# An attention stage on Trainium2: row maxima as 64-row tile pairs, in batches at the borders of scores and values

## The chip, the cores and the metric

The kernel runs on one core of a Trainium2 chip. A core has a matrix engine (TensorE, PE in the profile; PEld is its weight load), VectorE (DVE), ScalarE (ACT), GpSimd (POOL) and SyncE (SP), which here issues nearly all DMAs. Each engine works through its own instructions in order and waits on semaphores for the others. Operands lie in SBUF (128 partitions); matmul results lie in eight PSUM banks of 512 float32 per partition, and a bank must have been read before another matmul may use it. The metric is the device time of one execution in microseconds.

## The reference

One layer of a diffusion transformer on 2048 latent tokens and 256 context tokens, width 1024, in float32:

```python
sh1, sc1, g1, sh2, sc2, g2 = split(silu(c) @ w_mod + b_mod, 6)
h_x = rmsnorm(x, norm1_g) * (1 + sc1) + sh1
p_x = h_x @ w_in                      # k, v, q, u, vg, gate_a, gate_b
k_x, q_x = rope(rmsnorm(k)), rope(rmsnorm(q)) * 64 ** -0.5
s = q @ [k_ctx, k_x].T                # 8 heads of 64, 2 key/value heads, 2304 keys
attn = softmax(s) @ [v_ctx, v_x]
gm = gelu(u) * (gm_ws @ rmsnorm(gelu(vg)) + gm_bs)
x = x + g1 * ((sigmoid(ga) * (attn @ w_br_attn) + sigmoid(gb) * (gm @ w_br_gm)) @ w_out)
x = x + g2 * (relu(h2 @ w_ff1) ** 2 @ w_ff2)   # h2: rmsnorm of x, modulated by sh2, sc2
```

The context is projected to keys and values alone.

## The kernel before

The stages follow one another: the first part of the modulation (sh1, sc1), the projection (`project`, four blocks b of 512 tokens, up to about 780 us), the attention (`attend`, to about 1545), the merge of the branches with `w_out` (to about 1860) and the feed-forward part.

**Numbers in two parts.** A float32 factor is split into a high part that the format fp32r holds and the remainder, and a product is made of three matmuls (L155 to L157); `split` casts the high part (L123 on ACT, L125 on VectorE) and subtracts (L127). Weights come by DMA on SP (L435 in the projection), are split, and are then used.

**A unit of the attention** is a block b and a pair of heads p: 512 queries, two heads, 2304 keys in 18 key tiles j of 128. Scores stand transposed, keys on the partitions. Two matmuls make a score tile: `KA` (high part of the keys in rows 0 to 63, remainder in rows 64 to 127) with `qa` (the queries' high part, twice; L815), and `KB` (the high part in rows 0 to 63, a row of ones in row 64, zeros) with `qb` (the queries' remainder, and in row 64 minus the query's maximum; L816). So the exp (L818 on ACT) needs no bias. The values are float32 matmuls of the exps with the head's values, one head in columns 0 to 63 and one in 64 to 127 of one bank `o` (L826). The exps are added up over the key tiles on VectorE and POOL (L841, 512 columns each; L846 joins the two), and 16 matmuls with a column of ones turn the result into sums (L858), whose reciprocals (L863) are transposed (L866), copied and stored (L869) for the merge. `oc`, a copy of `o` (L850), is stored unscaled.

**Maxima** must be known before a unit's first score: `attn_prep` makes them one unit ahead, 40 matmuls (four query tiles, two heads, five key blocks; L770), each with one reduce on VectorE (L774), then their joint maximum (L779), its negative (L780) and the transposes for `qb` (L161, copied at L791).

**Order.** `attend` goes through three groups of six key tiles; after each score tile of a unit come three steps of the next unit's `attn_prep`, behind a group the values of the group before. At every sixth key tile one step of `mod_rest` (g1, sh2, sc2, g2: loads L280, multiply-adds L287 on VectorE, matmuls with ones L299 and L315) is put in; these are pinned. At its end `order` makes each tile of a pool wait for the program's previous tile of that pool (pools and their sizes: `POOLS`) and, in the attention, holds TensorE to the program's order; all else is ordered by a scheduler. Unit 0's maxima are made in the projection's tail, one step behind each piece of its last block.

## Time and profile before

| | |
|---|---|
| times of three runs, us | 3271.23, 3276.57, 3291.97 (median 3276.57) |
| profiled execution | 3275.92 us, its span 3274.1 us, mean clock of TensorE 0.979 |
| busy share of the span | PE 96%, DVE 61%, ACT 41%, POOL 30% |
| exps (L818, tiles in `pt`) | 480, 603 ns each |
| reduces of the maxima (L774) | 640, 627 ns each |
| adds of the exps on POOL (L841) | 272 of the commonest form, 1410 ns each |
| value matmuls (L826), records | 960 of the commonest form, 613 ns each |

A row of a group gives line, engine, operation, output<-input, shapes and count, then busy time and the mean duration in ns of one, then the engine's idle time just before and what ended it. A row of the timeline starts with the time from the span's start and the duration in us; "x3" joins neighbours, "[1.66 <-PE b L770]" is idle time and what ended it. SPq rows are DMA issues on SP.

### The profile page before, as it was taken

How to read it: one execution, taken by the hardware profiler on the slowest of the kernel's cores; microseconds unless marked ns; L12 is line 12 of the kernel's file. 1: busy time of each engine (PE TensorE's matmuls, PEld its weight loads, DVE VectorE, ACT ScalarE, POOL GpSimd, SP SyncE). 2: the span in 40 equal slices, each digit the busy share in tenths (PEclk: the TensorE clock that was granted, in tenths of full speed). 3: DMA queues.
4: the chain of work that ended last, by engine and by line, in shares of the span. 5: the costliest groups of instructions: out<-in, count | busy, mean ns of one | idle time of the engine just before them, and what ended most of it. 6: DMA issues, size and time to landing. Idle time of an engine off the chain costs nothing.

```text
span 3274.1 us, 38611 instructions
## 1 busy us (share of the span) xinstructions
PE 3127.4 (96%) x14100; PEld 2397.0 (73%) x14100; DVE 1987.0 (61%) x2910; ACT 1353.3 (41%) x2034; POOL 982.9 (30%) x672
## 2 busy tenths in 40 slices
PE   8999999999999999998799988999999899999999
PEld 4888887887555666664587766888778688888777
DVE  4736354556787888774433339887754676664555
ACT  3343534343444544453322216444543344443333
POOL 1423233334777887777633310000000000000000
PEclk9999999999999999999899998999999999999999
DMA  6353534342111111001555536989655634445564
GB/s 201 98 193 107 169 118 152 114 139 83 49 49 52 46 33 52 26 11 43 183 177 173 163 111 228 313 308 312 220 202 197 220 137 158 145 149 195 209 218 170
DMA packets 331838, 484.79 MB, mean 148 GB/s; under 512 B 33920, under 2 KB 166144, under 8 KB 331648
## 3 DMA queue, kind: packets, MB, share of 16 engines
q1 hardware_dynamic: 326032, 481.98, 44.0%
q8 instruction: 110, 1.80, 0.2%
q10 hardware_dynamic: 5616, 0.35, 0.1%
q14 instruction: 80, 0.66, 0.1%
HBM read 347.97 MB, written 134.28 MB: 147 GB/s over the span
## 4 chain that ended last, share of the span: by engine, by line
PE 76%; DVE 10%; DMA 5%; POOL 3%; issue 3%; ACT 2%; SPq 1%; ACTq 0%; DVEq 0%; POOLq 0%
PE b L1176 11%; PE b L1177 11%; PE b L1175 11%; PE b L157 7%; PE b L156 7%; PE b L155 7%; PE b L826 7%; PE b L770 4%; PE b L815 3%; PE b L816 3%; DVE ts L774 2%; PE b L161 2%; DMA f<-w2o_d 1%; DMA w<-in_w_in 1%; DVE f L1270 1%
## 5 line engine op out<-in xcount | busy, mean ns | idle before, releaser
L774 DVE TENSOR_REDUCE ts<-b 128x1 f32<-128x512 f32 (+1 forms) x640 | 357.4, 627 | 153.5 <-PE b L770 153.3
L841 POOL TENSOR_TENSOR t<-t,pt 128x512 f32<-128x512 f32 x272 | 376.5, 1410 | 137.2 <-ACT pt L818 134.6
L1261 DVE TENSOR_TENSOR f<-f,f 128x1024 fp32r<-128x1024 f32 x224 | 272.8, 1224 | 235.1 <-ACT f L1260 230.7
L1260 ACT CAST f<-f 128x1024 fp32r<-128x1024 f32 x224 | 235.0, 1051 | 381.8 <-DMA f<-ao_d 287.7
L1176 PE MATMUL b<-f,f 128*128 128x512 f32 x896 | 354.1, 395 | 15.2 <-DVE f L1261 14.7
L1177 PE MATMUL b<-h,f 128*128 128x512 f32 x896 | 350.0, 391 | 9.1 <-DVE f L1132 7.2
L1175 PE MATMUL b<-h,f 128*128 128x512 f32 x896 | 350.3, 392 | 4.8 <-ACT f L1131 4.3
L818 ACT ACTIVATE pt<-b 128x512 f32<-128x512 f32 x480 | 257.9, 603 | 227.0 <-PE b L816 221.7
L1177 PE MATMUL b<-f,f 128*128 128x512 f32 x896 | 351.1, 392 | 0.0
L1176 PE MATMUL b<-h,f 128*128 128x512 f32 x896 | 349.9, 391 | 0.0
L1175 PE MATMUL b<-f,f 128*128 128x512 f32 x896 | 306.6, 396 | 22.2 <-ACT f L1260 20.6
L127 POOL TENSOR_TENSOR w<-w,w 128x1024 fp32r<-128x1024 f32 x60 | 146.8, 2447 | 388.3 <-ACT w L123 152.0
L815 PE MATMUL b<-t,t 128*128 128x512 f32 x576 | 238.1, 413 | 0.0
L816 PE MATMUL b<-t,t 128*128 128x512 f32 x576 | 226.8, 394 | 0.0
L826 PE MATMUL b<-pt,t 128*64 128x512 f32 x960 | 223.3, 613 | 0.0
L123 ACT CAST w<-w 128x1024 fp32r<-128x1024 f32 x120 | 125.9, 1049 | 225.7 <-DMA w<-in_w_in 197.9
L1175 PEld LDWEIGHTS b<-f,f 128*128 128x128 f32 x896 | 168.7, 190 | 64.5 <-ACT f L1260 26.0
L1176 PEld LDWEIGHTS b<-f,f 128*128 128x128 f32 x896 | 169.8, 189 | 59.8 <-DVE f L1261 25.0
L155 PE MATMUL b<-t,w 128*128 128x512 f32 x512 | 203.2, 397 | 1.0 <-DVE t L568 1.0
L1177 PEld LDWEIGHTS b<-h,f 128*128 128x128 f32 x896 | 169.0, 189 | 45.9 <-DVE f L1132 7.9
L157 PE MATMUL b<-t,w 128*128 128x512 f32 x512 | 200.6, 392 | 0.0
L156 PE MATMUL b<-t,w 128*128 128x512 f32 x512 | 200.6, 392 | 0.0
(212 smaller groups left out, 6249.4 us busy)
## 6 DMA issues: line engine op xcount, KB each, us to landing
w<-in_w_in SPq DMA_DIRECT2D x120, 512.0 KB
ao_d<-f SPq DMA_DIRECT2D x224, 256.0 KB
f<-ao_d SPq DMA_DIRECT2D x112, 512.0 KB
f<-w2o_d SPq DMA_DIRECT2D x112, 512.0 KB
f<-in_w_ff SPq DMA_DIRECT2D x48, 1024.0 KB
w2o_d<-f SPq DMA_DIRECT2D x112, 256.0 KB
t<-in_w_mod SPq DMA_DIRECT2D x32, 512.0 KB
f<-x_d SPq DMA_DIRECT2D x64, 256.0 KB
```

What stands on the lines that cost most here:

```text
L155: mm(ps, sh, mh, start=start, stop=False)
L156: mm(ps, sh, ml, start=False, stop=False)
L157: mm(ps, sl, mh, start=False, stop=stop)
L774: nc.vector.tensor_reduce(out=mx[:, t, h, c : c + 1], in_=ps[:, :n], axis=AX.X, op=ALU.max)
L815: nc.tensor.matmul(s, self.KA[c][kv][:, ks], qa[h], start=True, stop=False)
L816: nc.tensor.matmul(s, self.KB[c][kv][:, ks], qb[h], start=False, stop=True)
L826: nc.tensor.matmul(o[0][h * HD : (h + 1) * HD, :], self.V[c][:, i, kv * HD : (kv + 1) * HD], pts[j][h], start=j == 0, stop=j == NKT - 1,)
L841: engs[e].tensor_tensor(out=accs[e][h], in0=first, in1=pt, op=ALU.add)
L1175: mm(ps, wh, hh, start=start and k == 0, stop=False, skip_group_check=True)
L1176: mm(ps, wh, hl, start=False, stop=False, skip_group_check=True)
L1177: mm(ps, wl, hh, start=False, stop=k == len(w) - 1, skip_group_check=True)
L1261: nc.vector.tensor_tensor(out=l, in0=f32(l), in1=f32(h), op=ALU.subtract)
```

## The change

- The maxima are made from the high parts alone (64 rows). A pair of matmuls makes one for each head: head 0 from rows 0 to 63 (`KA`), head 1 from rows 64 to 127 (`KB`, whose halves are swapped for it: the ones are in row 0, the keys in rows 64 to 127). A unit has 18 items (`todo`), two of which hold two half-wide pairs of the context's 256 keys; each fills two banks. `maxima(3)` takes three items: three borders of scores and values a unit, one batch before the values and one behind them.
- The scores' two matmuls of a key tile are called `first` and `second`; the exps of both heads lie in one tile of 2 × 512. In a unit's first group `low_queries` (the transposes for `qb`) stands behind the `first` of two key tiles.
- Key tiles 1, 4, 7 and 10 are added on VectorE, both heads in one instruction of 1024 columns; the others on POOL. `finish` joins the two on VectorE and makes the sums by two column-tiled matmuls with 64 columns of ones; row 0 of each half is stored (`sm_d`). Reciprocals are made once a block, on a packed tile that is loaded from `sm_d`, and stored to `rs_d`.
- `mod_rest` goes into the projection, a step behind each piece of a gate, with three tiles of its own (`md`); g1 is stored to DRAM and loaded again in `load_w_out`.
- VectorE is held to program order in the attention too. The pool `t2` has 46 tiles in place of 50.

```diff
-    "base": {"t4": 8, "t2": 50, "t1": 1, "ts": 12},
-    "front": {"w": 12, "m": 4},
-    "mid": {"pt": 21},
+    "base": {"t4": 8, "t2": 46, "t1": 1, "ts": 12},
+    "front": {"w": 12, "m": 4, "md": 3},
+    "mid": {"p2": 8, "ac": 4},
     "pre": {"in": 16, "raw": 2, "g1": 1},
     "join": {"bw": 14, "gt": 6, "y": 16, "wo": 18, "xt": 3, "jk": 2},
     "back": {"h": 56, "f8": 3, "f4": 12, "f2": 16, "fs": 5},
 }
 SLOTS = {tag: n for tags in POOLS.values() for tag, n in tags.items()}
 GROUP = 6
+ON_VECTOR = (1, 4, 7, 10)
...
-            acc = self.t4([D])
+            acc = self.sb("md", [D])
             for k in range(KC):
-                w = self.t4([D])
+                w = self.sb("md", [D])
                 nc.sync.dma_start(w, I["w_mod"][0, k * P : (k + 1) * P, lo : lo + D])
...
-                    self.g1b = dst
+                    nc.sync.dma_start(self.g1_d, dst[0:1])
...
                         self.gate_mm(h, b, c, wg, dst, m)
+                        next(mod, None)
...
-        nc.gpsimd.memset(z[HD:], 0.0)
-        nc.gpsimd.memset(z[HD : HD + 1], 1.0)
+        nc.gpsimd.memset(z[:HD], 0.0)
+        nc.gpsimd.memset(z[0:1], 1.0)
...
-                nc.vector.tensor_copy(kb[:HD, :n], f32(ka[:HD, :n]))
-                nc.scalar.copy(kb[HD:, :n], z[HD:, :n])
+                nc.vector.tensor_copy(kb[HD:, :n], f32(ka[:HD, :n]))
+                nc.scalar.copy(kb[:HD, :n], z[:HD, :n])
...
+        units[1].queries()
+        units[1].maxima(3)
...
+            for gi, g in enumerate(range(0, NKT, GROUP)):
+                group = range(g, g + GROUP)
+                if gi == 0:
+                    for j in group[:2]:
+                        u.first(j)
+                    if i:
+                        u.low_queries()
+                    for j in group[:2]:
+                        u.second(j)
+                for j in group[2 if gi == 0 else 0 :]:
+                    u.first(j)
+                    u.second(j)
+                    if j % GROUP == 2 and far:
+                        if gi == 0:
+                            far.load()
+                        elif gi == 2:
+                            far.queries()
+                    if not nxt:
                         next(late, None)
+                if nxt:
+                    nxt.maxima(3)
+                    if gi == 2:
+                        nxt.reference()
                 for f in pend:
                     f()
+                for f in after:
+                    next(f, None)
+                if gi == 0 and far:
+                    far.remainder()
+                step = nxt if gi < 2 else far
+                if step:
+                    step.maxima(3)
+                pend = [lambda u=u, j=j: u.values(j) for j in group]
+            pend.append(u.leave)
+            after = after[-1:] + [u.finish()]
...
+        self.g1b = self.sb("g1", [D])
+        nc.sync.dma_start(self.g1b, self.g1_d.partition_broadcast(P)[:, 0, :])
...
+            u = units[0]
+            u.load()
             yield from self.kb_build()
-            for i, _ in enumerate(self.attn_prep(0, 0, loaded.pop(0), qabs)):
-                if i == 30:
-                    loaded.append(self.attn_load(0, 1))
+            u.remainder()
+            yield
+            u.queries()
+            while u.todo:
+                u.maxima(1)
                 yield
-
-        prep0 = tail()
-        self.project(prep0)
+                yield
+            units[1].load()
+            units[1].remainder()
+            u.reference()
+            for _ in range(6):
+                yield
+            u.low_queries()
...
+            held = idx in pinned or (idx in fixed and i.engine in engines)
...
+        self.todo = [("ctx", t) for t in (0, 2)]
+        self.todo += [(c, t) for t in range(TT) for c in range(1, NB + 1)]
...
+    def maxima(self, n):
+        k, nc = self.k, self.nc
+        for _ in range(n):
+            if not self.todo:
+                return
+            c, t = self.todo.pop(0)
+            halves = ((0, slice(0, HD), k.KA), (1, slice(HD, P), k.KB))
+            ps = [k.bank([TB]) for _ in range(2)]
+            for s in range(2) if c == "ctx" else (0,):
+                tok = slice((t + s) * P, (t + s + 1) * P)
+                for h, rows, keys in halves:
+                    if c == "ctx":
+                        out, key = ps[h][:, s * CTX : (s + 1) * CTX], keys[0][self.kv]
+                    else:
+                        out, key = ps[h], keys[c][self.kv]
+                    nc.tensor.matmul(
+                        out, self.qa[h][rows, tok], key[rows, : out.shape[-1]],
+                        start=True, stop=True,
+                    )
+            for h in range(2):
+                if c == "ctx":
+                    nc.vector.tensor_reduce(
+                        out=self.mx[:, t : t + 2, h, 0:1],
+                        in_=ps[h].rearrange("p (s k) -> p s k", s=2), axis=AX.X, op=ALU.max,
+                    )
+                else:
+                    nc.vector.tensor_reduce(
+                        out=self.mx[:, t, h, c : c + 1], in_=ps[h], axis=AX.X, op=ALU.max
+                    )
+    def reference(self):
+        nm = self.k.small([TT, 2])
+        self.nc.vector.tensor_reduce(out=nm, in_=self.mx, axis=AX.X, op=ALU.max)
+        self.nc.vector.tensor_scalar(
+            out=self.pb[:, :, :, 0:1], in0=nm.unsqueeze(3), scalar1=-1.0, scalar2=None,
+            op0=ALU.mult,
+        )
+    def low_queries(self):
+        self.qb = self.turned(lambda t, h: self.pb[:, t, h, :])
...
+    def first(self, j):
+        k = self.k
+        c, _, ks = self.keys(j)
+        self.pts[j] = [k.bank([TB]) for _ in range(2)]
+        for h in range(2):
+            self.nc.tensor.matmul(
+                self.pts[j][h], k.KA[c][self.kv][:, ks], self.qa[h], start=True, stop=False,
+                skip_group_check=True,
+            )
+    def second(self, j):
+        k = self.k
+        c, _, ks = self.keys(j)
+        pt = k.t4([2, TB]) if j % GROUP >= GROUP - 2 else k.sb("p2", [2, TB])
+        for h in range(2):
+            s = self.pts[j][h]
+            self.nc.tensor.matmul(
+                s, k.KB[c][self.kv][:, ks], self.qb[h], start=False, stop=True,
+                skip_group_check=True,
+            )
+            self.nc.scalar.activation(pt[:, h], s, AF.Exp)
+        self.pts[j] = pt
+    def values(self, j):
+        k, nc = self.k, self.nc
+        c, i, _ = self.keys(j)
+        pt = self.pts.pop(j)
+        if j == 0:
+            self.o = k.bank([TB])
+        for h in range(2):
+            nc.tensor.matmul(
+                self.o[h * HD : (h + 1) * HD, :], k.V[c][:, i, self.kv * HD : (self.kv + 1) * HD],
+                pt[:, h], start=j == 0, stop=j == NKT - 1,
+            )
+        e = j in ON_VECTOR
+        old = self.acc.get(e)
+        if old is None:
+            self.acc[e] = pt
+            return
+        if e not in self.own:
+            self.own.add(e)
+            self.acc[e] = k.sb("ac", [2, TB])
+        if e:
+            nc.vector.tensor_tensor(out=self.acc[e], in0=old, in1=pt, op=ALU.add)
+        else:
+            for h in range(2):
+                nc.gpsimd.tensor_tensor(
+                    out=self.acc[e][:, h], in0=old[:, h], in1=pt[:, h], op=ALU.add
+                )
+    def leave(self):
+        k = self.k
+        oc = k.t2([TB])
+        self.nc.scalar.copy(oc, self.o)
+        self.nc.sync.dma_start(k.at_d[self.b][self.p * P : (self.p + 1) * P, :], oc)
+    def finish(self):
+        k, nc, b, p = self.k, self.nc, self.b, self.p
+        yield
+        a = self.acc[False]
+        nc.vector.tensor_tensor(out=a, in0=a, in1=self.acc[True], op=ALU.add)
+        yield
+        sm = k.bank([TB])
+        for h in range(2):
+            nc.tensor.matmul(
+                sm[h * HD : (h + 1) * HD, :], k.ones[:, :HD], a[:, h], start=True, stop=True
+            )
+        row = k.t2([TB])
+        nc.scalar.copy(row, sm)
+        for h in range(2):
+            nc.sync.dma_start(k.sm_d[b][2 * p + h : 2 * p + h + 1], row[h * HD : h * HD + 1])
+        if p + 1 == NH // 2:
+            n = NH * TT
+            r = k.t1([P])
+            pack = lambda d: d.rearrange("h (t c) -> (h t) c", c=P)
+            nc.sync.dma_start(r[:n], pack(k.sm_d[b]))
+            yield
+            nc.vector.reciprocal(r[:n], r[:n])
+            nc.sync.dma_start(pack(k.rs_d[b]), r[:n])
+        yield
```

Lines of the changed kernel that matter: maxima L1365 with reduces L1371 and L1376; `first` L1400, `second` L1411, exps L1415; values L1425; adds L1438 (VectorE) and L1441 (POOL); the join L1455, sums L1459, stores L1465, load L1470, reciprocal L1472, store L1473; transposes L174; modulation loads L289, multiply-adds L292 and L296.

TensorE at a border of scores and values, before: two key tiles of scores (L815, L816) with three maxima (L770) behind them, then the first values (L826) of the group before. Operands are output<-inputs; `b_` is a bank, `pt_` an exp tile, `t_` any tile of the pools.

```order
L815 MATMUL b_8737<-t_1615_8054,t_723_4093 128x512
L816 MATMUL b_8737<-t_1745_8448,t_1108_6291 128x512
L815 MATMUL b_8742<-t_1617_8061,t_723_4093 128x512
L816 MATMUL b_8742<-t_1747_8455,t_1108_6291 128x512
L770 MATMUL b_8747<-t_723_4093,t_1756_8504 128x512
L770 MATMUL b_8750<-t_983_5574,t_1756_8504 128x512
L770 MATMUL b_8753<-t_199_1119,t_1756_8504 128x256
L826 MATMUL b_8763<-pt_8485,t_133_672 64x512
L826 MATMUL b_8763<-pt_8490,t_133_672 64x512
```

The same border in the changed kernel, from the last rows of the values on (the six maxima of batch A stand the same way ahead of the values):

```order
L1425 MATMUL b_7086<-t_1268_6963,t_148_763 64x512 x2
L1425 MATMUL b_7086<-t_1271_6972,t_148_763 64x512 x2
L1365 MATMUL b_7108<-t_764_4214,t_1241_6885 128x512
L1365 MATMUL b_7109<-t_1154_6427,t_1243_6892 128x512
L1365 MATMUL b_7114<-t_1029_5711,t_1241_6885 128x512
L1365 MATMUL b_7115<-t_1158_6461,t_1243_6892 128x512
L1365 MATMUL b_7120<-t_203_1124,t_1241_6885 128x512
L1365 MATMUL b_7121<-t_1150_6415,t_1243_6892 128x512
L1400 MATMUL b_7126<-t_1161_6473,t_764_4214 128x512
L1400 MATMUL b_7127<-t_1163_6480,t_764_4214 128x512
L1411 MATMUL b_7126<-t_1233_6808,t_1154_6427 128x512
L1411 MATMUL b_7127<-t_1235_6815,t_1154_6427 128x512
```

No maxima stand between score tiles any more; six, each in a bank of its own, stand together.

VectorE at the start, where the rows h of block 0 are cast and split (`t_` tiles, L138 and L140; L125 and L127 before) and the modulation's g1 (`md_` tiles) is added up, in the changed kernel:

```order
L138 CAST t_70_503<-t_73_508 128x256
L140 TENSOR_TENSOR t_71_504<-t_73_508,t_70_503 128x256
L296 SCALAR_TENSOR_TENSOR md_1539<-md_1590,silu,md_1539 128x1024
L138 CAST t_74_512<-t_77_517 128x256
L140 TENSOR_TENSOR t_75_513<-t_77_517,t_74_512 128x256
L296 SCALAR_TENSOR_TENSOR md_1539<-md_1633,silu,md_1539 128x1024
L138 CAST t_78_521<-t_81_526 128x256
L140 TENSOR_TENSOR t_79_522<-t_81_526,t_78_521 128x256
```

Before, the casts and subtractions followed one another there, and all of L287 stood in the attention; SP issued no load of `w_mod` between those of `w_in`, where it now has this row:

```order
L444 DMA w_470<-in_w_in 128x4x256
L289 DMA md_1590<-in_w_mod 128x1024
L289 DMA md_1633<-in_w_mod 128x1024
L444 DMA w_476<-in_w_in 128x2x512
L289 DMA md_1699<-in_w_mod 128x1024
L289 DMA md_1742<-in_w_mod 128x1024
L444 DMA w_482<-in_w_in 128x2x512
```

SP's DMAs at the seam from the attention to the merge (`at_d` holds the outputs, `bw` is the first branch weight), before:

```order
L851 DMA at_d_91<-t_3305_13467 128x512
L869 DMA rs_d_2_286<-t_3353_13607 8x128
L851 DMA at_d_91<-t_3371_13701 128x512
L869 DMA rs_d_3_287<-t_3375_13717 8x128
L974 DMA bw_13725<-in_w_br_attn 128x4x128
```

And in the changed kernel:

```order
L1465 DMA sm_d_276<-t_2959_13031 1x512 x2
L1449 DMA at_d_91<-t_2960_13059 128x512
L1465 DMA sm_d_276<-t_2962_13066 1x512 x2
L1470 DMA t_2963_13070<-sm_d_276 32x128
L1473 DMA rs_d_280<-t_2963_13070 32x128
L849 DMA bw_13079<-in_w_br_attn 128x4x128
```

The load of the sums (L1470) and the store of their reciprocals (L1473) now stand between the last sums and the branch weight.

More of the change, by code (lines that the diff above doesn't have):

```diff
@@ L112, in small, with psum, bank @@
         return self.sb("fs" if "back" in self.open_pools else "ts", shape, dtype)
-    def bank(self, shape, dtype=F32):
+    def psum(self, banks):
+        if self.banks:
+            self.psum_stack.close()
+        self.banks = banks
+        self.psum_stack = ExitStack()
+        self.psp = self.psum_stack.enter_context(
+            self.tc.tile_pool(name="ps", bufs=1, space=PSUM, reuse_waits="tile")
+        )
+    def bank(self, shape, dtype=F32, tag="b"):
         self.uid += 1
-        t = self.psp.tile([P] + list(shape), dtype, tag="b", name=f"b_{self.uid}")
-        self.tags[t.name] = "b"
+        t = self.psp.tile(
+            [P] + list(shape), dtype, tag=tag, name=f"{tag}_{self.uid}", bufs=self.banks[tag]
+        )
+        self.tags[t.name] = tag
         return t
@@ L167, in constants @@
         dp = ec(self.tc.tile_pool(name="spill", bufs=1, space=DRAM))
-        self.psp = ec(self.tc.tile_pool(name="ps", bufs=8, space=PSUM))
+        self.psum({"b": 8})
         self.ident = cp.tile([P, P], F32, name="ident")
@@ L205, in constants @@
         self.wo_d = operands("w2o")
-        self.rs_d = [
-            [
-                dp.tile([2 * TT, P], F32, tag=f"rs{b}_{p}", name=f"rs_d{b}_{p}")
-                for p in range(NH // 2)
-            ]
-            for b in range(NB)
-        ]
+        self.g1_d = dp.tile([1, D], F32, tag="g1", name="g1_d")
+        self.sm_d = spill("sm", [NH, TB])
+        self.rs_d = spill("rs", [NH, TB])
         self.open("base")
@@ L888, in kb_build, with attend @@
             self.KB.append(KB)
[L890 to L893 removed]
+    def attend(self, units, late):
         begin = self.here()
[L895 removed]
+        pend, after = [], []
+        units[1].queries()
+        units[1].maxima(3)
         for i, u in enumerate(units):
[L897 to L914 removed]
@@ L925, in attend @@
+                if gi == 0 and far:
[6 more added lines that the diff above has]
+            after = after[-1:] + [u.finish()]
         for f in pend:
             f()
-        for _ in after:
-            pass
-        for _ in side:
-            pass
-        self.pe_pins.append(range(begin, self.here()))
+        for f in after:
+            for _ in f:
+                pass
@@ L933, in load_w_out @@
+        self.fixed.append(range(begin, self.here()))
     def load_w_out(self):
@@ L1386, in build @@
         late = self.br_inputs(0, first)
-        self.attend(qabs, prep0, loaded, self.mod_rest(), late)
+        self.attend(units, late)
         self.merge(first, late)
```

239 lines of the change are left out of this document (63 added, 176 removed).

## The prediction

> **What bounds the kernel now.** I began with the page's busy shares, then read the windows by stage, since a share of the whole span hides that the stages have different limits. In a window's row stand its length, then the busy time of PE, PEld, DVE, ACT and POOL, the granted clock, the DMA share and GB/s.
>
> ```profile
> span 3274.1 us, 38611 instructions
> PE 3127.4 (96%) x14100; PEld 2397.0 (73%) x14100; DVE 1987.0 (61%) x2910; ACT 1353.3 (41%) x2034; POOL 982.9 (30%) x672
> 30.00:40.00 10.00, 6.97 (x17) 1.27 (x16) 5.09 (x19) 3.98 (x8) 0.00 (x0) 1.00 1.05 391
> 50.00:60.00 10.00, 9.51 (x79) 9.19 (x78) 9.83 (x17) 7.67 (x12) 4.75 (x2) 0.98 0.20 60
> 400.00:600.00 200.00, 196.07 (x952) 164.91 (x951) 94.41 (x195) 81.12 (x114) 62.96 (x33) 0.98 0.43 135
> 1030.00:1080.00 50.00, 49.68 (x236) 31.73 (x236) 37.78 (x56) 23.73 (x46) 36.86 (x29) 0.97 0.14 37
> 1400.00:1500.00 100.00, 99.27 (x478) 61.39 (x476) 76.61 (x112) 49.11 (x93) 78.23 (x59) 1.00 0.03 9
> 1500.00:1600.00 100.00, 78.01 (x324) 49.59 (x325) 31.82 (x31) 34.74 (x62) 73.72 (x50) 0.90 0.38 123
> 1900.00:2200.00 300.00, 270.92 (x1194) 223.09 (x1193) 221.08 (x318) 135.75 (x203) 1.16 (x1) 0.94 0.73 248
> ```
>
> The projection (400 to 600) and the attention (1030 to 1080, 1400 to 1500) are bound by TensorE: it is busy 98% and 99% of them, at a clock of 0.97 to 1.00. So PE work that goes is a gain if no wait takes its place, and PE work that comes costs its full length. The start is another matter: from 50 to 60 us VectorE is busy 9.83 of 10. The two copies of an attention output that lie 13 units apart give the length of a unit (one block, one pair of heads): (1469.07 − 843.6)/13 = 48.1 us.
>
> ```profile
> L850 ACT COPY t<-b x16: 586/587/587, 843.6 to 1540.1; 128x512 f32<-128x512 f32 x16
> 1469.07 0.59 ACT L850 COPY t<-b 128x512 f32<-128x512 f32 x1 [5.26 <-PE b L826]
> ```
>
> **The unit's PE work, before.** A pitch (start to start) is what a matmul costs in a row of them; its duration also holds what overlaps with the next.
>
> ```profile
> 914.90 1.88 PE L299 MATMUL b<-t,ones 128*128 128x512 f32 x4
> 916.85 0.40 PE L816 MATMUL b<-t,t 128*128 128x512 f32 x1
> ...
> 1204.38 1.09 ACT L818 ACTIVATE pt<-b 128x512 f32<-128x512 f32 x2 [5.57 <-PE b L816]
> 1204.59 0.85 PE L770 MATMUL b<-t,t 128*128 128x512 f32 x3
> 1205.02 5.21 DVE L774 TENSOR_REDUCE ts<-b 128x1 f32<-128x512 f32 x9 [1.66 <-PE b L770]
> 1205.27 0.39 PE L815 MATMUL b<-t,t 128*128 128x512 f32 x1
> ...
> 1213.01 1.04 PE L161 MATMUL b<-ident,t 128*128 128x128 f32 x8
> 1213.98 4.51 PE L826 MATMUL b<-pt,t 128*64 128x512 f32 x20
> 1218.32 1.03 PE L826 MATMUL b<-t,t 128*64 128x512 f32 x4
> 1219.28 0.50 PE L815 MATMUL b<-t,t 128*128 128x512 f32 x1
> ```
>
> Three maxima take 1205.27 − 1204.59 = 0.68, so 0.2275 each, and a score matmul, fp32r like them, the same. A unit has 72 score matmuls (16.4 us) and 32 maxima of 512 keys and 8 of 256 (at half, 0.12): 8.2 us. A key tile's values, a pair on two column halves, leave four records (float32 leaves two each) and take (1218.32 − 1213.98)/5 = 0.87; six tiles and the change of shape behind them 5.3, three times, less 0.1 each: 15.5. Sixteen transposes at (1213.98 − 1213.01 − 0.1)/8 = 0.109 are 1.75, the sums 1.95 or less (L858, below). With 0.5 of modulation that is 44.2 in a unit of 48.1; the clock and small stalls make the rest.
>
> **The unit after.** The maxima (L1365) are 16 pairs of 512 and 4 of 256, each a matmul on rows 0 to 63 and one on rows 64 to 127. No row here shows two row halves at once. The bounds are one pitch a pair (16 × 0.2275 + 4 × 0.12 = 4.1 us) and two (8.2, nothing gained). The nearest row is the value pair: L299, one float32 matmul over all columns, also leaves two records and takes (916.85 − 914.90 − 0.23)/2 = 0.86, so a pair of column halves takes the time of one full matmul. I take the same for row halves, and the serial case as a rival. The sums (L1459) become one such column pair: 0.86 for 1.75. So 16.4 + 4.1 + 15.5 + 1.75 + 0.86 = 38.6 us.
>
> Then the waits. All maxima now stand at the three borders of a unit as batches of three pairs: A ahead of the values, B behind them. A batch fills six of eight PSUM banks at once, and VectorE, held to program order, empties them.
>
> ```profile
> L774 DVE TENSOR_REDUCE ts<-b 128x1 f32<-128x512 f32 x463 | 290.6, 680 | 110.7 <-PE b L770 110.6
> L841 POOL TENSOR_TENSOR t<-t,pt 128x512 f32<-128x512 f32 x249 | 344.7, 1410 | 134.5 <-ACT pt L818 132.0
> L287 DVE SCALAR_TENSOR_TENSOR t<-t,silu,t x28: 1275/1869/2298, 798.8 to 1335.3; 128x1024 f32<-128x1024 f32 x28
> L780 DVE TENSOR_SCALAR t<-ts 128x8 f32<-128x8 f32 x15 | 14.4, 959 | 1.2
> L742 DVE TENSOR_TENSOR t<-t,t 128x512 f32<-128x512 f32 x14 | 10.4, 743 | 0.0
> ```
>
> Nine reduces took 5.21, a pitch of 0.6 (they start 1205.02 − 1204.59 = 0.43 behind the first matmul), so a batch occupies VectorE for 3.6. Its new adds of 1024 (L1438, L1455) have no row; the nearest is L287, two inputs of 1024 beside POOL's adds: 1.27 to 2.30, median 1.87, which I take. B's first pair comes 0.7 (A) + 5.3 + two changes of shape (0.1 each) + 0.1 = 6.3 behind A's, so its reduce could start at 6.7.
> - Border 0: A, then the remainder (0.74, as L742). VectorE is in time. The next scores want two banks a key tile every 0.91, the reduces free two in 1.2: about 0.3 lost.
> - Border 1: A, two adds: VectorE is free at 0.43 + 3.6 + 3.74 = 7.8, so 0.6 to 1.1 late; with 0.3 for the banks, 1.1.
> - Border 2: A, reference (1.2: L780 and a reduce of 40 elements at some 0.2), two adds: 9.0, against 7.8 (the sums' 0.9 and a shape more); 1.2 late. Here `low_queries` follows after four score matmuls; its second set of transposes waits for the sixth bank (5 × 0.6 + 0.43 + 1.2 = 4.6, where PE is there at 0.7 + 0.9 + 0.44 = 2.1), and a copy (0.6, an estimate from the 0.62 of an ACT cast of 512, below) stands before the second score matmuls: 3.1 in all.
>
> Together 4.5. At the end of the scores A waits for exps: ACT needs 1.09/2 = 0.545 for one, PE 2 × 0.2275 = 0.455, twelve times, so ACT ends two banks behind; 0.3 to 0.4 at each border, 1.0. Changes of shape: 12 a unit for 6, at 0.1 (the last value pair starts at 1218.32 + 0.43, the score 0.53 later): 1.2 in all, between none and 3.6, if a row shape cost three times that. POOL's 26 adds at 1.41 are 37 us of 46: not the bound. Sum 38.6 + 4.5 + 1.0 + 1.2 = 45.3, at the clock of 0.97 46.7; 1.4 less than 48.1, for 15 units **−21**.
>
> A rule speaks against all these changes of shape: the Trainium skill, "TensorEngine Tiling (Array Packing)", Key Properties, says that changing the tiling mode drains TensorE. The trace agrees, at 0.1 us between values and scores; by the rule six more drains a unit cost 0.6, without it nothing, 9 us over 15 units.
>
> **Outside the attention.** Rest of the modulation: its matmuls (L299 and L315) leave the attention, where they stood in the 48.1, and go into a projection that is 98% PE.
>
> ```profile
> 1208.49 1.84 PE L315 MATMUL b<-ones,t 128*128 128x1 f32 x16
> 1542.01 1.95 PE L858 MATMUL b<-ones,t 128*128 128x1 f32 x16 [1.96 <-POOL t L846]
> ```
>
> 2 × 1.84 + 4 × 0.86 = **+7**; its VectorE adds lie under a VectorE that is half idle (94.41 of 200). If weight loads on SP queue behind modulation loads that wait for VectorE, up to 5 more; nothing if PE's 2% of gaps took them.
>
> The start: the order puts the g1 part there, eight loads of 512 KB on SP among the projection's weights, and seven of its adds on VectorE among the casts of h.
>
> ```profile
> 52.84 0.38 PE L155 MATMUL b<-w,t 128*128 128x256 f32 x1 [0.49 <-ACT t L418]
> 65.49 0.41 DVE L125 CAST t<-t 128x512 fp32r<-128x512 f32 x1
> 67.31 0.58 PE L157 MATMUL b<-w,t 128*128 128x256 f32 x1 [0.55 <-POOL t L127]
> ```
>
> PE waits at 67.31 for POOL, which works behind that cast, and VectorE is full before it (9.83 of 10). Seven at L287's fastest, 1.27 (POOL adds little there), are 8.9; PE's own work to 60 us covers about one: **+8**. Low end 4, if half lie in waits that are there; high end 15, seven at 1.87 and SP late: each modulation load beyond the pool's three waits for VectorE, with the weights queued behind it, and DMA is full until 40 us (1.05, 391 GB/s; 4 MB more are 10 us).
>
> Unit 0's maxima, 40 matmuls for 20 pairs in the projection's tail: 4.1 less; **−3** (0 to −4).
>
> The seam to the merge:
>
> ```profile
> 1544.26 0.27 PE L866 MATMUL b<-ident,ts 128*8 128x128 f32 x1 [0.30 <-DVE ts L863]
> 1544.89 0.28 SPq L869 DMA_DIRECT2D rs_d<-t  x1
> 1545.27 0.38 SPq L974 DMA_DIRECT2D bw<-in_w_br_attn  x1
> 1547.91 0.62 ACT L123 CAST bw<-bw 128x512 fp32r<-128x512 f32 x1 [3.04 <-DMA bw<-in_w_br_attn]
> 1553.25 0.79 PE L155 MATMUL b<-in,bw 128*128 128x512 f32 x1 [8.72 <-ACT bw L123]
> ```
>
> PE waits 8.72 us for the first branch weight, whose load SP issues right behind the store of the sums. Now SP has the two row stores, the load that must see them land, and a store behind VectorE's reciprocal ahead of it: two landings at 2.6 us (the load issued at 1545.27 was cast from 1547.91), less the 0.9 that go from the sums' end (1542.01 + 1.95) to the store at 1544.89, less 1 us of sums: **+3** (0 to 6). The reload of g1 (L811) is read only at the first residual: nothing, or one such landing, within that 6.
>
> The pool of 46 slots for 50 I cost at nothing: the projection's other PE work (98% busy) covers a late slot; uncovered, a tile of 512 waits for its reader a few times, 3 us.
>
> Sum against the profiled execution, 3275.9 (span 3274.1): 8 + 7 − 3 − 21 + 3 = −6, so **3270**. The median of the runs is 0.7 above it; I leave that out.
>
> **The rivals.**
> 1. Faster: VectorE is never late (its adds at 1.27, where POOL leaves it alone) and the waits of 4.5 and 1.0 shrink to about 2. The unit is 41.8/0.97 = 43.1, −75 over 15: 3216. For it: L287's median is 1.87, but its fastest, 1.27, is what one costs undisturbed. Against: POOL is busy 36.86 of 50 in the attention. 0.20.
> 2. Slower, the clock: PE with 5 to 6 us of gaps in 46 gets less of it. Where PE is busy 90% and 78% above, the clock is 0.94 and 0.90; at 0.92 the unit is 45.3/0.92 = 49.2, +17 for 15, so 3308; with adds of 2.30 at the borders (1.3 more) 3329. It decides where PE's busy share falls below about 92%, in the border waits. Against: 0.97 at 99% shows that the share is not all. Beside it stands the skill's "TensorE: Matmul & The Clock Gate": its Part 1 lets the clock fall after an idle window of some 3.4 us, and these waits are 3.1 at most; but "A second HAM failure mode: psum-queue depth-cycling" tells of just such short gaps between groups that wait for banks, and speaks against the change. No trace here shows which. 0.27.
> 3. The change does not do what it says: the row halves go one behind the other. PE then has 4.1 more a unit, but slower matmuls lie in part under VectorE's lag at the borders (of six batches, the three B's hide most): +2 a unit, 30 in all and 3 in the tail: 3303. 0.13.
> 4. My case, 0.40.
>
> **How the numbers follow.** The likeliest case's own range, with ±1.5 a unit (23) and the ends of the other terms: 3240 to 3300. Rivals 1 and 2 hold 0.47 between them, so the range goes from below rival 1's 3216 to rival 2's upper 3329: 3212 to 3328. A measurement of this kernel tells some 1% (33 us). Faster by more (under 3243): rival 1 and 0.05 of my case, 0.25. Slower by more (over 3309): two thirds of rival 2 (0.18), half of rival 3 with a start at its high end (0.06), 0.05 of my case: 0.29. The rest, 0.46, within 1%.
>
> **What would show it.** In the changed profile: copies of the outputs (L1448) 46.7 apart; pair matmuls that start together or within a few ns; VectorE's first reduce of B about 1 us behind its matmul at borders 1 and 2, and PE's longest wait of a unit behind the transposes of `low_queries`; a granted clock of 0.97 between 800 and 1500; the first projection matmuls some 8 us later than at 52.8 to 67; about 12 us from the last sums to the first branch matmul. A clock below 0.94 in the attention, pairs a pitch apart, or adds of 1.3 would make it wrong.

## The result, and the profile after

The changed kernel took 3318.55 us in the median of four runs (3309.98 to 3321.78), the kernel before 3279.73 beside it: a ratio of 1.011, interval 1.007 to 1.015. I had forecast 3270 in a range of 3212 to 3328: the time lies in the range, on the side of slower, where I had forecast a small gain. The page of the changed kernel, and three windows with the columns as in the prediction:

```profile
span 3314.4 us, 38022 instructions
PE 3116.7 (94%) x13892; PEld 2333.5 (70%) x13892; DVE 1951.5 (59%) x2770; ACT 1344.3 (41%) x2034; POOL 969.0 (29%) x672
50.00:60.00 10.00, 1.32 (x9) 1.05 (x10) 8.98 (x13) 2.66 (x5) 2.22 (x2) 0.64 0.64 217
400.00:600.00 200.00, 196.30 (x949) 164.11 (x948) 105.51 (x213) 86.24 (x117) 63.15 (x33) 0.99 0.48 149
1030.00:1080.00 50.00, 47.14 (x218) 25.17 (x218) 34.31 (x46) 24.56 (x48) 38.11 (x30) 1.00 0.04 12
```

TensorE is busy for 10.7 us less and the span is 40.3 longer: new waits. From 50 to 60 us TensorE has 1.32 us of work, where it had 9.51; in the attention it is busy 94% in place of 99%, at a full granted clock. The copies of the outputs give the stages, as before:

```profile
L1448 ACT COPY t<-b x16: 586/587/589, 880.6 to 1579.5; 128x512 f32<-128x512 f32 x16
1501.42 0.59 ACT L1448 COPY t<-b 128x512 f32<-128x512 f32 x1 [5.40 <-PE b L1425]
1542.60 0.59 ACT L1448 COPY t<-b 128x512 f32<-128x512 f32 x1 [2.82 <-PE b L1425]
1592.35 0.79 PE L168 MATMUL b<-in,bw 128*128 128x512 f32 x1 [12.03 <-ACT bw L136]
```

A unit is (1501.42 − 880.6)/13 = 47.8 us, mostly 47.6. By equal events of the two traces, the 40.3 us arise so:

| stretch | I had said | measured |
|---|---|---|
| start, to block 0's first gates | +8 | +12.5 |
| projection, to block 3's gates at 715 us | +7 | +19.3 |
| tail and first unit, to the first copy | −3 | +5.2 |
| 13 units, first to 14th copy | −18 | −4.6 |
| last two units | −3 | +7.0 |
| seam and after | +3 | +0.9 |

**The start.** VectorE in the changed kernel, then the same copy of block 0's first key block in the kernel before:

```profile
48.08 1.28 DVE L296 SCALAR_TENSOR_TENSOR md<-md,silu,md 128x1024 f32<-128x1024 f32 x1
65.50 1.28 DVE L296 SCALAR_TENSOR_TENSOR md<-md,silu,md 128x1024 f32<-128x1024 f32 x1 [1.33 <-DMA md<-in_w_mod]
79.61 0.41 DVE L512 COPY t<-b 128x256 f32<-128x256 f32 x1
```

```profile
65.83 0.41 DVE L503 COPY t<-b 128x256 f32<-128x256 f32 x1
```

The adds have the length I took (1.28), and VectorE waits for a load once (1.33). The chain of casts, on which TensorE waits, is 13.8 later here.

**The projection.** The border of blocks 0 and 1 in the timeline of the changed kernel:

```profile
252.65 0.33 SPq L289 DMA_DIRECT2D md<-in_w_mod  x1
253.56 0.38 SPq L444 DMA_DIRECT2D w<-in_w_in  x1
256.21 0.28 PE L169 MATMUL b<-w,t 128*128 128x256 f32 x1
256.33 0.28 PE L170 MATMUL b<-w,t 128*128 128x256 f32 x1
257.20 1.29 DVE L296 SCALAR_TENSOR_TENSOR md<-md,silu,md 128x1024 f32<-128x1024 f32 x1 [2.38 <-DMA md<-in_w_mod]
259.25 1.04 ACT L136 CAST w<-w 128x1024 fp32r<-128x1024 f32 x1 [6.09 <-DMA w<-in_w_in]
261.50 1.56 DVE L138 CAST t<-t 128x512 fp32r<-128x512 f32 x1 [3.01 <-ACT t L427]
263.11 0.58 PE L168 MATMUL b<-w,t 128*128 128x256 f32 x1 [5.06 <-DVE t L138]
267.20 0.41 PE L169 MATMUL b<-w,t 128*128 128x256 f32 x1
267.42 0.41 PE L170 MATMUL b<-w,t 128*128 128x256 f32 x1
```

SP issues the weight's load behind a modulation load that had to wait for a tile; ScalarE, in order, stands 6.09 us at the cast of that weight, with the activation (L427) behind it that TensorE's next h needs. TensorE stands 5.06 us and then works at a pitch of 0.21 for 0.12 until about 271.4 (the granted clock from 263 to 272 is 0.54), which is another 3 us.

**A border of the attention.** TensorE and VectorE at border 1 of a unit, and two of the four groups of VectorE's adds of 1024 (the other two, also L1438, have 1808 and 2120 ns):

```profile
1227.54 0.96 PE L1365 MATMUL b<-t,t 64*128 64x512 f32 x6
1228.43 0.50 PE L1400 MATMUL b<-t,t 128*128 128x512 f32 x1
1230.10 0.50 PE L1400 MATMUL b<-t,t 128*128 128x512 f32 x1 [1.16 <-DVE ts L1376]
...
1225.45 1.77 DVE L1438 TENSOR_TENSOR ac<-p,t 128x1024 f32<-128x1024 f32 x1
1227.14 2.30 DVE L1455 TENSOR_TENSOR ac<-ac,ac 128x1024 f32<-128x1024 f32 x1
1229.36 3.67 DVE L1376 TENSOR_REDUCE ts<-b 128x1 f32<-128x512 f32 x6
...
L1438 DVE TENSOR_TENSOR ac<-ac,p 128x1024 f32<-128x1024 f32 x13 | 30.8, 2369 | 0.0
L1455 DVE TENSOR_TENSOR ac<-ac,ac 128x1024 f32<-128x1024 f32 x13 | 29.9, 2298 | 0.0
```

Batch B's six matmuls take 0.89 with the change of shape, so the row halves run side by side (one behind the other they would need 6 × 0.2275 = 1.37); in the records the two of a pair start 3 to 4 ns apart. Its first reduce could start at 1227.97 and starts at 1229.36: 1.4 late, behind the two adds; the score matmul at 1230.10 waits for the bank.

**The last unit.** VectorE, then TensorE:

```profile
1563.32 1.75 DVE L837 TENSOR_TENSOR raw<-raw,raw 128x512 f32<-128x512 f32 x1 [3.65 <-DMA raw<-rs_d]
1566.66 2.28 DVE L1438 TENSOR_TENSOR ac<-p,t 128x1024 f32<-128x1024 f32 x1
1568.87 2.28 DVE L1455 TENSOR_TENSOR ac<-ac,ac 128x1024 f32<-128x1024 f32 x1
1571.29 1.98 PE L1459 MATMUL b<-ac,ones 128*64 128x512 f32 x4 [5.35 <-DVE ac L1455]
```

VectorE, held to program order, waits for the loads of the merge's inputs (L837, four times some 3.6 us) ahead of the adds that the sums need.

### The profile page after: what moved, and what is told of

Read it like the earlier page. It is cut to its first block, busy times and chain, and to the rows that moved or that the text cites. A ratio compares the mean times of both kernels' runs of the same rounds, so it can differ in the third digit from the quotient of the medians.

```text
span 3314.4 us, 38022 instructions
## 1 busy us (share of the span) xinstructions
PE 3116.7 (94%) x13892; PEld 2333.5 (70%) x13892; DVE 1951.5 (59%) x2770; ACT 1344.3 (41%) x2034; POOL 969.0 (29%) x672
## 4 chain that ended last, share of the span: by engine, by line
PE 66%; DVE 17%; DMA 8%; POOL 3%; ACT 3%; issue 3%; SPq 1%; DVEq 0%; ACTq 0%; POOLq 0%
PE b L1051 11%; PE b L1052 11%; PE b L1050 11%; PE b L170 6%; PE b L168 6%; PE b L169 6%; PE b L1400 4%; PE b L1411 4%; DVE ts L1376 3%; PE b L1425 3%; DVE ac L1438 3%; DMA w<-in_w_in 2%; PE b L1365 2%; PE b L174 2%; DMA f<-w2o_d 1%
## 5 line engine op out<-in xcount | busy, mean ns | idle before, releaser
L1376 DVE TENSOR_REDUCE ts<-b 128x1 f32<-128x512 f32 x512 | 314.5, 681 | 246.4 <-PE b L1365 246.4
L1441 POOL TENSOR_TENSOR ac<-ac,p 128x512 f32<-128x512 f32 x256 | 323.6, 1300 | 106.5 <-ACT p L1415 106.5
L140 POOL TENSOR_TENSOR w<-w,w 128x1024 fp32r<-128x1024 f32 x60 | 149.0, 2483 | 418.8 <-ACT w L136 242.2
L1415 ACT ACTIVATE p<-b 128x512 f32<-128x512 f32 x384 | 201.0, 618 | 152.9 <-PE b L1411 150.4
L1400 PE MATMUL b<-t,t 128*128 128x512 f32 x576 | 205.6, 423 | 37.4 <-DVE ts L1371 17.3
L1441 POOL TENSOR_TENSOR ac<-ac,t 128x512 f32<-128x512 f32 x128 | 208.7, 1654 | 0.0
L168 PE MATMUL b<-w,t 128*128 128x512 f32 (+1 forms) x528 | 193.5, 367 | 12.0 <-ACT t L427 6.9
```

Source lines behind the costliest of these rows:

```text
L168: mm(ps, sh, mh, start=start, stop=False)
L1376: nc.vector.tensor_reduce(out=self.mx[:, t, h, c : c + 1], in_=ps[h], axis=AX.X, op=ALU.max)
L1400: self.nc.tensor.matmul(self.pts[j][h], k.KA[c][self.kv][:, ks], self.qa[h], start=True, stop=False, skip_group_check=True,)
L1415: self.nc.scalar.activation(pt[:, h], s, AF.Exp)
L1441: nc.gpsimd.tensor_tensor(out=self.acc[e][:, h], in0=old[:, h], in1=pt[:, h], op=ALU.add)
```

## The experiments

All are edits of the changed kernel. The stretch behind the last copy, whose work is the same in all, took 1734 to 1743 us from one profile to the next, so a change of a few microseconds in an early stage is read at the copies, and the medians beside them.

| run | median, us | ratio to the kernel before, interval |
|---|---|---|
| changed kernel | 3318.55 | 1.011 (1.007 to 1.015) |
| modulation left out | 3290.97 | 1.005 (1.003 to 1.006) |
| adds behind batch B | 3278.75 | 1.001 (1.000 to 1.002) |
| maxima spread | 3314.22 | 1.012 (1.010 to 1.015) |
| VectorE not held | 3353.43 | 1.024 (1.022 to 1.026) |
| modulation held | 3334.87 | 1.017 (1.015 to 1.020) |
| held and paced | 3315.47 | 1.011 (1.009 to 1.014) |
| merge's inputs over two units | 3315.64 | 1.012 (1.010 to 1.014) |
| three edits | 3276.87 | 1.001 (0.999 to 1.002) |
| four edits | 3248.06 | 0.991 (0.989 to 0.992) |
| tail | 3315.57 | 1.012 (1.010 to 1.013) |
| held, one load | 3299.16 | 1.006 (1.005 to 1.008) |

### What the modulation costs

```diff
-        prep0, mod = tail(), self.mod_rest()
+        prep0, mod = tail(), iter(())
+        for dst in (self.S2, self.G2, self.g2b):
+            nc.vector.memset(dst, 0.5)
+        g1 = self.sb("md", [D])
+        nc.vector.memset(g1, 0.5)
+        nc.sync.dma_start(self.g1_d, g1[0:1])
```

> The rest of the modulation (loads, multiply-adds, matmuls for g1, sh2, sc2, g2) is left out and constants stand in its place; all else is the changed kernel. Theory M (the trace read so: 12.5 us at the start and 19 in the projection are the modulation's, 7 of them PE work and the rest waits of the queues): 32 us less than the changed kernel's 3318, so about 3286, and the first key copy of block 0 back at 66 us. Rival S (only my own terms, 8 and 7, are its price; the rest of the lost time comes from the maxima in the projection's tail): 15 less, 3303.

The first copy came 30.5 us earlier than in the changed kernel (6.5 later than before, for 37.0), the median fell by 27.6. That is near theory M's 32, not the 15 of my terms; the tail's loss stayed (3.3 behind before at the gate piece of 715 us, 10.6 at 735). The first key copy of block 0 came at 68.87, not back at 66 (65.83 before; 66.25 in the held run below): some 3 us at the start were lost here without the modulation too, and why is not shown.

### The order of adds and maxima on VectorE

```diff
-ON_VECTOR = (1, 4, 7, 10)
+ON_VECTOR = (4, 5, 10, 11)
...
                 step = nxt if gi < 2 else far
                 if step:
                     step.maxima(3)
+                done = u if gi else (units[i - 1] if i else None)
+                if done:
+                    done.adds()
```

`adds` makes the additions that stood in `values`; the join of `finish` follows it. The edit also changes which key tiles VectorE adds, not how many, so its effect is that of the order and the choice together.

> VectorE's adds of the exps stand behind batch B in its order in place of ahead of it (key tiles 4, 5, 10, 11 in place of 1, 4, 7, 10 on VectorE, same number), all else as changed. Theory V (the border waits come from VectorE being late for B behind two adds): units of about 45.5 for 47.6, 30 us less over 15 units, 3288. Rival B (the waits come from six banks filling at once, late or not): units of 47 to 47.6, within 8 us of 3318.

Units of 45.0, 2.6 less each and 36 over the 13 (by the copies), 39.8 less in the median: theory V, and more than it said. VectorE at a border:

```profile
1205.05 3.68 DVE L1384 TENSOR_REDUCE ts<-b 128x1 f32<-128x512 f32 x6 [2.58 <-PE b L1373]
1208.64 2.33 DVE L1456 TENSOR_TENSOR ac<-t,t 128x1024 f32<-128x1024 f32 x1
1210.90 2.31 DVE L1473 TENSOR_TENSOR ac<-ac,ac 128x1024 f32<-128x1024 f32 x1
```

VectorE now waits for the matmuls of B (2.58), and not they for it. The adds, as long as before, lie beside the scores.

### Batches or one by one

```diff
                 for j in group[2 if gi == 0 else 0 :]:
                     u.first(j)
                     u.second(j)
+                    if nxt:
+                        nxt.maxima(1)
...
-                if nxt:
-                    nxt.maxima(3)
...
```

> No batches: one item of maxima (a pair of row halves) behind each of the 18 key tiles of a unit, so 36 changes of tile shape around maxima for 12, and two banks at a time; all else as changed. Theory B (the batches make the waits, a change of shape costs 0.1 us): units of 38.6 + 3.6 + about 1.5 = 43.7, 58 us less over 15 units, about 3260. Rival D (a change to row tiles drains TensorE at 0.3 or more): 49 or more a unit, 3340.

Units of 47.4: neither 43.7 nor 49. No wait of TensorE for VectorE is left, and still next to nothing is won:

```profile
1206.11 0.73 PE L1398 MATMUL b<-t,t 128*128 128x512 f32 x2
1206.68 0.62 PE L1409 MATMUL b<-t,t 128*128 128x512 f32 x2
1207.23 0.49 PE L1363 MATMUL b<-t,t 64*128 64x512 f32 x2
1207.66 0.74 PE L1398 MATMUL b<-t,t 128*128 128x512 f32 x2
...
1200.00:1300.00 100.00, 99.52 (x434) 47.13 (x435) 70.87 (x92) 48.55 (x88) 76.21 (x58) 1.00 0.04 12
```

A key tile and a pair take 1.55 us, where five pitches of 0.2275 are 1.14: the two changes of shape cost 0.41 together, so 0.21 each, not 0.1. Of the 0.41, 0.1 stands ahead of the pair, 0.2 behind it, and 0.1 behind the first full matmul (1206.11 to 1206.68 is 0.57 for two pitches, 0.455). That last part I had overlooked in the kernel before as well. Behind the values the first score matmul, at 1219.28, is followed by

```profile
1219.62 0.39 PE L816 MATMUL b<-t,t 128*128 128x512 f32 x1
```

so 0.34 later for a pitch of 0.2275: with the 0.1 ahead of it, a change from column tiles to full ones costs 0.21 too. So theory B has the place right and the price of its cure wrong; the batches are the better form, once VectorE is there for them. By the Trainium skill, "TensorEngine Tiling (Array Packing)", Key Properties, a change of the mode drains TensorE; the trace agrees, at some 0.2 us for each of these changes.

### VectorE not held to program order

```diff
-        engines = (self.nc.tensor.engine, self.nc.vector.engine)
+        engines = (self.nc.tensor.engine,)
```

> VectorE is not held to program order in the attention (the scheduler orders it, TensorE stays held), all else as changed. Theory H (in the last unit VectorE stands before loads of the merge's inputs, with the last adds behind them): the interval from the last copy but one to the last falls from 36.9 us to about 30, 7 us less; the units in between as the scheduler has the adds, 0 to 20 us less: 3290 to 3311. Rival P (the last unit waits for POOL's adds, whose order does not change): no change in that interval.

The last interval fell to 28.0, as H said. The other units grew to 50, which I had not expected: the scheduler put the join (L1455) ahead of batch B.

```profile
1221.56 1.23 DVE L1455 TENSOR_TENSOR ac<-ac,ac 128x1024 f32<-128x1024 f32 x1 [6.08 <-POOL ac L1441]
1223.01 2.48 DVE L1371 TENSOR_REDUCE ts<-b 128x2 f32<-128x512 f32 x4
...
1223.75 1.99 PE L1400 MATMUL b<-t,t 128*128 128x512 f32 x3 [3.61 <-DVE ts L1371]
...
1200.00:1300.00 100.00, 91.58 (x408) 50.09 (x406) 60.25 (x88) 44.89 (x86) 72.13 (x55) 0.95 0.04 12
```

The join waits for POOL, B's reduces behind it, TensorE 3.61 us; and the granted clock is 0.95, where the changed kernel with its shorter waits (1.2) has 1.00.

### Where the modulation's steps stand, and their loads

Held to their places, then held and fewer:

```diff
+                        at = self.here()
                         next(mod, None)
+                        self.pins.append(range(at, self.here()))
```

> Each step of the rest of the modulation is held to its place behind a piece of a gate, so that none of it is put at the start; same number of steps, all else as changed. Theory Q (the start's 12.5 us are the adds among the casts of h and go; the projection's wait comes from loads that stand in one queue with the weights, and stays at 19 or grows by the steps that come in): first norm of block 0 back within 1 us of before, and the kernel 8 to 13 us below 3318. Rival G (the same work costs the same wherever it stands): no change of over 3 us.

```diff
-                        next(mod, None)
+                        piece = c * 4 + i * 2 + m
+                        if piece % 2 == 0 or piece == 15:
+                            at = self.here()
+                            next(mod, None)
+                            self.pins.append(range(at, self.here()))
```

> As the run with held steps, but a step only behind every second piece of a gate, nine a block over all four blocks, so that a load has twice the time. Theory Q: the waits of the queue in the projection go from about 12 to 4, PE's 7 stay: 20 us below 3318, 3298. Rival W (what it costs is DMA traffic and VectorE work, not the pace): as the run with held steps within 4 us.

Held: the start was within 0.4 us of before, so Q's first half stands; but block 3 began 46.4 late for 32.1, and the kernel was 16 us slower, a miss of both theories. A held load no longer runs ahead, and the matmul that uses the sum is held too. Paced: 22.8 late at block 3, so pace counts and W falls; but nine steps now stood in block 3 with the tail, where 10 us were lost, and the median fell by 3 only, not 20. To tell loads from adds, the held form with one load in place of 32:

```diff
-                w = self.sb("md", [D])
-                nc.sync.dma_start(w, I["w_mod"][0, k * P : (k + 1) * P, lo : lo + D])
+                w = self.g2b
+                if c == 0 and k == 0:
+                    nc.sync.dma_start(w, I["w_mod"][0, k * P : (k + 1) * P, lo : lo + D])
```

> The run with held steps, with one load of the modulation's weights in place of 32 (the multiply-adds and matmuls stay, on the same slice, so the modulation's values are wrong). Theory Q (TensorE waits for loads that are late, in one queue with the weights): of the 46 us that the held steps had cost by block 3, some 10 stay (PE's 7 and a little), so 3335 - 36 = 3299. Rival V (VectorE's multiply-adds themselves are late or delay the casts): 3325 or more.

3299, as theory Q had it: 9.9 late at block 3. What TensorE waited for between 80 and 720 us (us in all, times, the longest), in the held run, and then with one load:

```profile
PE b L308 <- DVE md L296: 13.5, 2, 8.0
PE b L324 <- DVE md L296: 12.0, 2, 8.3
```

```profile
PE b L325 <- DVE md L297: 2.0, 1, 2.0
```

The adds and matmuls are the same in both, so 23.5 us of wait go with the loads. The other 13 of the 36.5 by which block 3 begins earlier agree with the granted clock between 80 and 720 us, 0.97 in the held run and 0.99 with one load (2% of 640 us, an estimate). That the loads are late because they stand in one queue with the weights, and not by the traffic itself (154 GB/s in that stretch, 134 with one load), is read from the order of issue above and not shown; a second queue was not tried.

### The tail

```diff
+            for _ in range(7):
+                yield
             u.queries()
+            for _ in range(7):
+                yield
             while u.todo:
```

> Only the projection's tail is changed: seven steps (one piece of a gate) of distance before and behind unit 0's query transposes. Theory T (TensorE stands 3 us there because the copies of the transposes wait on ScalarE behind the key copies, and then runs slower for some us): the last pieces of block 3's gates 6 to 7 us earlier, 3312. Rival U (other waits of the tail take its place): within 2 us of 3318.

The wait that stood in the changed kernel's tail, and what is left of it:

```profile
764.03 1.70 PE L1365 MATMUL b<-t,t 64*128 64x256 f32 x8 [2.98 <-ACT t L1340]
```

```profile
PE b L1369 <- ACT t L1344: 0.4, 1, 0.4
```

The first copy came 9.2 us earlier. Of these, 2.6 stood at block 3's first key copy already (29.5 late for 32.1), ahead of the steps that were moved, so the tail is worth some 7: theory T. The median fell by 3.0 only; in the profiled execution 2.6 went in the last unit and 6 behind the last copy, and of those 6 I can show no cause.

### The merge's inputs, and the edits together

```diff
-                    if not nxt:
+                    if i + 2 >= len(units) and j % GROUP in (1, 4):
                         next(late, None)
```

> The steps that load and split the merge's inputs are spread over the last two units, every third key tile, in place of one behind each key tile of the last unit; VectorE stays held to program order; all else as changed. Theory H: the last interval between copies falls from 36.9 to 30, 7 us below 3318: 3311. Rival P (POOL's adds set the end of the last unit): no change.

The last interval fell from 36.9 to 28.0, so H holds and P falls; the one before it rose from 41.2 to 44.6, the median fell by 3. Together with the adds behind B and the paced steps:

> Three edits together: adds behind batch B, the modulation's steps held and paced, the merge's inputs spread over two units. If the three costs are separate, 3279 - 20 - 7 = 3252, which is 0.7% below the kernel before. If they hide one another (the same wait counted twice), 3265 or more.

This is the second case (3265 or more): the kernel equals the one before. The trace names what ate the rest: 17 us late at block 3, 11 more in the tail, and 48.9 for the last interval but one (41.2 in the changed kernel). So each was given its own remedy: eleven steps a block with the matmul a step later, the tail's distance, and the merge's inputs one step at each border, behind the adds:

> Four edits together: adds behind batch B; eleven held steps of the modulation a block, their matmuls one step later than the last add; a piece of a gate between unit 0's query transposes and its first maxima; one step of the merge's inputs at each border of the last four units, behind the adds. If each wait was its own: 3277 for the three edits before, less 6 (tail), 4 (merge's inputs), 3 (modulation): about 3264, 0.4% below the kernel before. If the waits only move (VectorE or SP late elsewhere): 3272 or more.

```profile
span 3246.5 us, 38060 instructions
```

The kernel takes 3248.06, 0.9% below the kernel before (0.8 to 1.1) and some 2% below the changed one: block 3 begins 10.9 late, the tail loses nothing (10.0 at its last gate), units are 45.0, the last interval 28.0. It beats both kernels, by more than I expected of it.

## Why the prediction was right or wrong

Between the −6 that I forecast and the +40 that came lie 46 us: 13 in the units of the attention, 12 in the projection, 10 in the last two units, 8 in the tail, 4.5 at the start, and 2 the other way behind the last copy.

**The work of the unit** was right: the row pairs run side by side, the sums are one column pair, and TensorE's busy time fell. So rival 3 falls, and rival 1 with the length of the adds (1.81 to 2.37 in the mean, where it needs 1.27). **Rival 2** falls too: the granted clock was 1.00 in most windows of the attention, above the 0.97 I had taken. The page that spoke for the rival, "A second HAM failure mode: psum-queue depth-cycling" in the Trainium skill's "TensorE: Matmul & The Clock Gate", does not describe this kernel, whose waits for banks are 1.2 us, two in a unit, at a clock of 1.00; the page's Part 1, an idle window of some 3.4 us, agrees with the wait of 5.06 us and the slow pitch behind it, and with 0.95 in the run with one wait of 3.6 to 4.5 in each unit.

**The borders** hold the first terms that were mis-sized, and all three were too small: 4.5 us of waits for banks, 1.0 of waits for exps, 1.2 of changes of shape. By the starts of TensorE's matmuls, in the mean of the 13 units, they are 5.5 (0.3, 1.8 and 3.4 behind batch B of borders 0, 1 and 2, where I had 0.3, 1.1 and 3.1), 1.4 and 2.3, which make the 9.2 of 47.8 − 38.6. I named the lateness of VectorE behind the adds; at border 1 it was 1.4 (I had 0.6 to 1.1). Its four adds of 1024 took 1.81, 2.30, 2.37 and 2.12 for the 1.87 that I took from L287. POOL's adds beside them are a likely reason, not a shown one: with VectorE not held, the join, which there waits for POOL, takes 1.23, but some adds among POOL's take 1.20 too. For the changes of shape I had read 0.1, the part ahead of the first matmul, and left out the 0.1 behind it. The full clock gave some of it back. So a unit won 0.4 us for 1.4 (47.75 for 48.11).

**The projection** is the step that failed: "2 × 1.84 + 4 × 0.86 = +7 ... up to 5 more". The 7 is about what stays when the loads are out of the way (9.9 with one load). The other 10 to 12 go with the loads, by their place in the queue as far as the order of issue tells: I saw that weight loads stand behind modulation loads that wait for a tile, and gave it up to 5 without following one weight to the cast, the activation behind the cast on ScalarE, and TensorE. **The start** was right in kind and length of the adds (7 × 1.28 = 9). It was short by one wait for a load (1.3) and by longer waits of the casts for ScalarE (2.6 in all for 0.7).

**The tail** and **the last unit** I had not looked at: −3 and −3, where +5 and +7 came. In both a wait stood in an order that had been harmless: the transposes' copies behind the key copies on ScalarE, with the maxima now directly behind them; and the merge's inputs ahead of the adds on a VectorE that had not been held to program order before. I wrote of VectorE's order at the borders, and not of what else the new order catches. **The seam** with all that follows cost 0.9 where I had 3, within its range: TensorE's wait for the first branch weight grew as I had it (12.03 for 8.72), but the sums ahead of it are shorter and no longer wait 1.96 for POOL, so from the last copy to the first branch matmul it is 12.85 us for 13.12.

So the sign was decided by waits, each of the size of the gain: adds behind B are worth 36 us, the modulation 30.5 of which some 10 are needed, the tail some 7, all at the copies. The 0.29 that I gave to slower by over 1% stood mostly on the clock; slower came by another way.

## What to carry to other kernels

Where an engine is newly held to program order, list everything that now stands in that order and waits for a DMA or a slower engine, not only the work that the change is about. Batches of matmuls that fill the banks are cheap if their reader is free when they start; put the reader's other work behind them. Where loads that must wait for a tile are put among others on one queue, follow the next of the others to its user before calling the move free. And read the price of a change of shape up to the second matmul behind it.

## What the runs showed that I had not expected

A change between full tiles and 64-row tiles costs some 0.2 us each way, half of it behind the first matmul of the new shape; counted so, the change from column tiles to full ones costs as much. A single pair among scores pays it twice, 0.41 a key tile, which makes single pairs little better than late batches (47.4 and 47.6). After a wait of 5.06 us TensorE worked for 8 us at a pitch of 0.21 in place of 0.12, so the wait cost 8 us in all, while waits of 1.2 left the granted clock at 1.00.
